# Gathered rows used a block later, two U blocks more ahead of the W build, and gated rows on ScalarE, in a decoder block with product-key experts

## The chip, the cores and the metric

The kernel runs on one core of a Trainium2 chip. The metric is the device time of one execution in microseconds (us), the median over several executions. One more execution was recorded by the hardware profiler; every row below is of that one.

## What is computed

One decoder layer over 512 tokens of width 1024, all float32: a normalisation, two token mixers side by side (differential attention and a chunked mLSTM), an output projection, and then a feed-forward part with 16,384 single-neuron experts. Each of 8 heads scores the token against two sets of 128 keys, takes the best 16 of each, combines them, keeps the best 16 of the sums, and weighs those experts by a softmax. The change concerns this last part:

```python
def peer_ffn(h, w_q, sub_keys, U, V):
    q = (h @ w_q).reshape(T, 8, 2, 128)
    # 16 best keys of each half, 16 best pairs -> eidx (expert numbers), gate (softmax of the scores)
    ...
    act = gelu(einsum('td,thkd->thk', h, U[eidx]))
    y = einsum('thk,thkd->td', act * gate, V[eidx])
```

U and V have 16,384 rows of 1024 numbers; expert number = 128 * (first key) + (second key).

## The kernel before

**Two ways to the same sum.** The first 128 tokens (block 0) have their rows of U and V fetched: there are 128 slots a token, so 128 gathers of U rows and then 128 of V rows, each an indirect DMA that brings one row of 4 KB to each of the 128 partitions (`gather`, L925, issued by GpSimd, POOL in the profile). VectorE (DVE) uses each gathered tile with one instruction of 128x1024: L931 multiplies it with the tokens' rows of h (`hrow`) and adds up to one number of `act`; L941 adds act times the row to the output `yg`. The gathered tiles lie in five rooms (`NGB`, tag "g").

The other 384 tokens are computed densely, over all experts, in 128 steps n1 of 128 experts each. `up(n1)` loads a U block of 512 KB by SP's queue (`raw_U`), ScalarE (ACT) makes its rounded high half `hi_U` (L991), DVE the rest `lo_U` (L992), TensorE (PE) makes 24 matmuls "act" (L1000 to L1002), and ACT takes their gelu into `ga` (L1004). Then the V block of the same step is loaded and split (`hi_V`, `lo_V`, L138), `ga` is multiplied by the block's gates W (L1031) and split (`ahi`, `alo`), and PE makes 18 matmuls "y" (L1046) that add to six sums in PSUM. `NGA` is 32: so many `ga` tiles exist, so that U blocks can run ahead of the V blocks.

**The gates W.** Before any y can start, the gates must be spread into W, which has a number for each token and expert. That is done in 48 blocks (`build_w`): DVE makes `onehot` (L867) and `gated` (L871), each 128x2048 in f16. One half of `gated` holds the high part of the gate in the place of the key, the other half the low part. PE makes 16 matmuls `wps` (L876, L877) of them, and ACT brings the result to a tile `st` and, for the first keys, to W0 (L883, L882). `st` goes to memory, and W comes back from there piecewise (L1025, SP's queue). While W is built, PE's free time goes to U blocks.

**The gathers' pace.** In `up`, a copy of one column of `lo_U` on POOL (`pace`, L994) stands ahead of the gathers that belong to this step (`gstep`, from n1 = 16 on 256 gathers over 111 steps, 2.3 a step); they are issued after it.

**What sets the order.** The program is written with tiles. A scheduler orders each engine's instructions once, when the program is built; on the chip each engine runs its list in that order, and waits for data and for rooms. A tag's `bufs` says how many rooms its tiles share: a tile that takes a room waits for the last reader of the tile before it.

**The rows of h.** Ahead of the scores of the keys, `hrow` is made at L892 to L896: DVE adds the halves of h (`hs4`), PE transposes four tiles, ACT copies to `hrow`, twice. `hs4` lies in one of the two rooms of tag "qt", which next hold `qt`, the transposed queries (L767), from which PE makes the key scores `pkeys` (L770), from which DVE takes the best 16 (`top16`, L753 to L757). `jcol` (L739) is a list 0 to 127 that POOL's iota makes; DVE casts it (L740, L742).

## Time and profile before

| | |
|---|---|
| Time, median of 3 runs | 1936.19 us (1936.87, 1919.65, 1936.19) |
| Profiled execution: its own time | 1931.02 us |
| Its span, first to last instruction | 1929.2 us |
| PE busy | 1814.1 us (94%) |
| DVE busy | 1428.4 us (74%) |
| ACT busy | 811.1 us (42%) |
| POOL busy | 685.8 us (36%) |
| Chain that ended last | PE 58%, DVE 18%, DMA 9%, ACT 5%, issue 5%, POOL 4% |
| Mean granted TensorE clock | 0.978 |

The busy shares are averages over stages with different limits. The feed-forward part begins near 643 us; its key scores and selections fill 650 to 800 us, the W build with the first U blocks about 800 to 957 us, and the V blocks with the remaining U blocks and all gathers the rest. A row of the chain that ended last tells who released whom, back from the last instruction.

### The profile page before, as it was taken

What the parts mean: (1) busy time and instruction counts of PE and PEld (TensorE: products, weight loads), DVE (VectorE), ACT (ScalarE), POOL (GpSimd) and SP (SyncE); (2) the same over time, 40 slices, a digit from 0 to 9 for tenths busy, and PEclk for the clock granted to TensorE, in tenths of its full rate; (3) what the DMA queues carried; (4) which work ended last, traced back from release to release, by engine and by line L of the source; (5) the groups of instructions that cost most, each with busy time, mean ns of one, the idle gap of its engine ahead of it and who ended that gap; (6) DMA issues with size and microseconds to landing.
All of it is one profiled execution on the core that took longest, in us unless ns stands there. A gap on an engine that the chain in (4) does not pass through costs nothing.

```text
span 1929.2 us, 28915 instructions
## 1 busy us (share of the span) xinstructions
PE 1814.1 (94%) x10751; PEld 1632.3 (85%) x10751; DVE 1428.4 (74%) x2732; ACT 811.1 (42%) x1359; POOL 685.8 (36%) x608
## 2 busy tenths in 40 slices
PE   5999899899998998999699999999999899999997
PEld 4989799798986888999688888899898788888886
DVE  7664746645556799999889888887776667776777
ACT  5565464463562423555434333333333233333332
...
GB/s 283 129 69 81 138 59 158 112 63 148 71 88 98 75 102 99 117 239 247 265 302 153 339 355 349 317 337 336 323 285 247 276 299 274 273 295 246 321 283 132
DMA packets 160283, 404.26 MB, mean 210 GB/s; under 512 B 14471, under 2 KB 63368, under 8 KB 160142
## 3 DMA queue, kind: packets, MB, share of 16 engines
...
HBM read 373.52 MB, written 28.84 MB: 209 GB/s over the span
## 4 chain that ended last, share of the span: by engine, by line
PE 58%; DVE 18%; DMA 9%; ACT 5%; issue 5%; POOL 4%; SPq 0%; DVEq 0%; POOLq 0%; ACTq 0%
PE y L1046 20%; PE act L1002 7%; PE act L1000 7%; PE act L1001 7%; DMA gath<-V,idx 4%; DMA ada_w<-ada_w 3%; POOL gath L925 2%; DVE lo_U L992 2%; DVE ada_acc L219 1%; DVE lo_V L138 1%; PE wps L876 1%; PE wps L877 1%; DVE ga L699 1%; ACT p L489 1%; DVE gm L701 1%
## 5 line engine op out<-in xcount | busy, mean ns | idle before, releaser
L1002 PE MATMUL act<-h_hi,lo_U 128*128 128x384 f32 x1024 | 347.1, 339 | 16.9 <-DVE lo_U L992 16.7
L1000 PE MATMUL act<-h_hi,hi_U 128*128 128x384 f32 x1024 | 345.0, 337 | 2.6 <-ACT ga L1004 2.2
L1001 PE MATMUL act<-h_lo,hi_U 128*128 128x384 f32 x1024 | 344.3, 336 | 0.0
L994 POOL COPY pace<-lo_U 128x1 f32<-128x1 f32 x128 | 99.9, 782 | 572.8 <-DVE lo_U L992 572.1
L941 DVE SCALAR_TENSOR_TENSOR yg<-gath,act,yg 128x1024 f32<-128x1024 f32 x127 | 163.0, 1283 | 111.2 <-DMA gath<-V,idx 110.6
L1046 PE MATMUL y<-lo_V,ahi 128*128 128x512 f32 x762 | 241.2, 397 | 2.6 <-DVE lo_V L138 2.6
L137 ACT CAST hi_V<-raw_V 128x1024 fp32r<-128x1024 f32 x128 | 134.3, 1050 | 245.9 <-PE y L1046 207.3
L1046 PE MATMUL y<-hi_V,alo 128*128 128x512 f32 x762 | 233.9, 395 | 1.0 <-DVE alo L138 1.0
L1046 PE MATMUL y<-hi_V,ahi 128*128 128x512 f32 x762 | 222.4, 397 | 6.0 <-ACT ahi L137 4.2
L925 POOL DMA_INDIRECT gath<-U,idx x128 | 177.1, 1383 | 130.1 <-DVE junk L931 99.3
L1002 PEld LDWEIGHTS act<-h_hi,lo_U 128*128 128x128 f32 x1024 | 192.8, 188 | 25.3 <-DVE lo_U L992 20.6
L1000 PEld LDWEIGHTS act<-h_hi,hi_U 128*128 128x128 f32 x1024 | 192.9, 188 | 8.5 <-ACT ga L1004 3.1
L1001 PEld LDWEIGHTS act<-h_lo,hi_U 128*128 128x128 f32 x1024 | 192.7, 188 | 4.3
L138 DVE TENSOR_TENSOR lo_V<-raw_V,hi_V 128x1024 fp32r<-128x1024 f32 x128 | 155.8, 1219 | 41.9 <-ACT hi_V L137 39.0
L991 ACT CAST hi_U<-raw_U 128x1024 fp32r<-128x1024 f32 x128 | 134.2, 1049 | 111.4 <-PE act L1001 98.6
L137 ACT CAST ahi<-ga 128x384 fp32r<-128x384 f32 x127 | 65.0, 512 | 271.0 <-DVE ga L1031 140.3
L1046 PEld LDWEIGHTS y<-hi_V,alo 128*128 128x128 f32 x762 | 142.5, 187 | 35.4 <-DVE alo L138 1.9
L1046 PEld LDWEIGHTS y<-lo_V,ahi 128*128 128x128 f32 x762 | 142.8, 188 | 35.0 <-DVE lo_V L138 3.6
L992 DVE TENSOR_TENSOR lo_U<-raw_U,hi_U 128x1024 fp32r<-128x1024 f32 x128 | 156.4, 1222 | 19.4 <-ACT hi_U L991 13.3
L1046 PEld LDWEIGHTS y<-hi_V,ahi 128*128 128x128 f32 x762 | 142.0, 189 | 33.3 <-ACT ahi L137 4.8
L925 POOL DMA_INDIRECT gath<-V,idx x128 | 149.4, 1167 | 35.3 <-issue 31.5
L931 DVE SCALAR_TENSOR_TENSOR junk<-gath,hrow 128x1024 bf16<-128x1024 f32 x128 | 156.0, 1219 | 4.4 <-DMA gath<-U,idx 3.5
...
## 6 DMA issues: line engine op xcount, KB each, us to landing
raw_U<-UT SPq DMA_DIRECT2D x128, 512.0 KB
raw_V<-V SPq DMA_DIRECT2D x128, 512.0 KB
...
```

The source lines that it names most:

```text
L137: A.copy(hi, src)
L138: eng.tensor_tensor(lo, src, hi.bitcast(F32), op=OP.subtract)
L925: G.indirect_dma_start(out=t_, out_offset=None, in_=src, in_offset=bass.IndirectOffsetOnAxis(ap=idx0[:, s:s + 1], axis=0))
L931: V.scalar_tensor_tensor(junk2, u, 1.0, hrow, op0=OP.mult, op1=OP.mult, accum_out=act[:, s:s + 1])
L941: V.scalar_tensor_tensor(yg, v, act[:, s:s + 1], yg, op0=OP.mult, op1=OP.add)
L991: A.copy(hi, raw)
L992: V.tensor_tensor(lo, raw, hi.bitcast(F32), op=OP.subtract)
L994: with tc.issue_after(G.tensor_copy(pace, lo[:, 0:1].bitcast(F32)).ins):
L1000: T.matmul(ps, hi[:, ks], h_hi[:, k], start=(k == 0), stop=False)
L1001: T.matmul(ps, hi[:, ks], h_lo[:, k], start=False, stop=False)
L1002: T.matmul(ps, lo[:, ks], h_hi[:, k], start=False, stop=(k == KD - 1))
L1046: T.matmul(ys[d][j], l[:, tsl], r[:, j * 512:(j + 1) * 512], start=(m == 0 and i == 0), stop=(m == KEYS - 1 and i == 2))
```

## The change

It has three parts.

**Later use.** `up` no longer uses a gathered tile where it is gathered. Tiles are put on a list `landing`, and are used in the next call of `up`, behind that block's `lo_U` in DVE's order. Tag "g" gets a sixth room (`NGB` 6).

**Two more U blocks ahead.** The gelu results of U blocks 0 and 1 no longer take two of the 32 `ga` rooms, but lie in the 4 KB room that `hrow` had (`ga01`). The rows of h go to memory instead: `hrow_out` takes a room of tag "qt", and two DMAs on ACT's queue write it to `hrow_dram` (256 KB each); one DMA on SP's queue loads it back at n1 = 2, once both `ga01` tiles have been read. `jcol` moves to tag "qt", too.

**ScalarE makes low rows.** In every fourth of the 48 W blocks (b % 4 == 2, 12 of them), DVE makes the high half of `gated` alone (128x1024), and ACT makes the low half in 8 instructions of 128x128, each a multiplication by a column of `glo`. `glo` is made by one more DVE instruction of 128x128 for each of 3 token blocks.

```diff
--- before.py
+++ after.py
@@ -41,7 +41,7 @@
     (O_QA + hp * 256,), (O_KA + hp * 256,), (O_VA + hp * 256,), (O_QM + hp * 128, O_KM + hp * 128),
     (O_VM + hp * 256,), (O_OM + hp * 256,), (O_GM + hp * 256,), (O_GA + hp * 256,))]
 NGA = 32
-NGB = 5
+NGB = 6
 QB = 1
 RB = 6
 STB = 2
@@ -719,11 +719,12 @@
     W_dram = dram.tile([NB, P, KEYS - NR, WB], F32, name="W_dram")
 
     dp = ctx.enter_context(tc.tile_pool(name="dense", bufs=1))
-    hrow = dp.tile([P, D], F32, name="hrow")
+
+    ga01 = dp.tile([P, D], F32, tag="hrow", bufs=1, name="ga01")
     idx0 = dp.tile([P, NS], I32, name="idx0")
     gate0 = dp.tile([P, NS], F32, name="gate0")
+    hrow_dram = dram.tile([P, D], F32, name="hrow_dram")
     s0_dram = dram.tile([P, NH, 2, KEYS], F32, name="s0_dram")
-    jcol = dp.tile([P, KEYS], I32, name="jcol")
 
     off_c, doff_c, iota_c = [dp.tile([P, TOPK], F16, name=n) for n in ("off_c", "doff_c", "iota_c")]
     w0pool = ctx.enter_context(tc.tile_pool(name="w0", bufs=1, side="right"))
@@ -736,6 +737,7 @@
     n21T = rp.tile([P, XT // TB, 2, TB, 2], F16, name="n21T")
     ghl = rp.tile([P, XT // TB, 2, TB, 2], F16, name="ghl")
     iota16 = rp.tile([P, KEYS], F16, name="iota16")
+    jcol = rp.tile([P, S], F32, tag="qt", bufs=2, name="jcol").bitcast(I32)[:, 0:KEYS]
     G.iota(jcol, pattern=[[1, KEYS]], base=0, channel_multiplier=0)
     V.tensor_copy(iota16, jcol)
     iota_rep = bc(iota16[:, None, :], [P, 2 * TB, KEYS])
@@ -853,12 +855,18 @@
             V.tensor_copy(n21T[:, bs, 1 - i], bc(src[:, :, :, None], [P, P // TB, TB, 2]))
         gp = bc(ps[:, 2 * P:3 * P].rearrange("p (b t) -> p b t", t=TB)[:, :, :, None], [P, P // TB, TB, 2])
         V.tensor_scalar(ghl[:, bs, 0], gp, GS, None, op0=OP.mult)
+        glo[t] = rp.tile([P, P], F32, tag="glo", bufs=2, name="glo")
+        V.scalar_tensor_tensor(glo[t].rearrange("p (b t) -> p b t", t=TB), ps[:, 2 * P:3 * P].rearrange(
+            "p (b t) -> p b t", t=TB), GS, ghl[:, bs, 0, :, 0], op0=OP.mult, op1=OP.subtract)
         V.scalar_tensor_tensor(ghl[:, bs, 1], gp, GS, ghl[:, bs, 0], op0=OP.mult, op1=OP.subtract)
 
+    glo = {}
+
     def build_w(t):
 
 
-        for b in range((t - DBS[0]) * P // TB, (t + 1 - DBS[0]) * P // TB):
+        cs0 = (t - DBS[0]) * P
+        for b in range(cs0 // TB, (cs0 + P) // TB):
             tag, dt = (("w_hi1", F32R), ("w_lo1", F32R), ("w_raw1", F32))[b % 3 if b < 2 * NB - RB else b % 2]
             pairs = [wpool.tile([P, D], dt, tag=tag, bufs=2, name=n).bitcast(F16).rearrange(
                 "p (a t n) -> p a t n", a=2, t=TB) for n in ("onehot", "gated")]
@@ -868,9 +876,13 @@
                             iota_rep.rearrange("p t (n u) -> p t n u", u=2),
                             bc(n21T[:, b].rearrange("p a t u -> p (a t) u")[:, :, None, :], [P, 2 * TB, KEYS // 2, 2]),
                             op=OP.is_equal)
-            V.tensor_tensor(pairs[1].rearrange("p a t (n u) -> p a t n u", u=2),
-                            bc(e1.rearrange("p t (n u) -> p t n u", u=2)[:, None], [P, 2, TB, KEYS // 2, 2]),
-                            bc(ghl[:, b][:, :, :, None, :], [P, 2, TB, KEYS // 2, 2]), op=OP.mult)
+            na = 1 if b % 4 == 2 else 2
+            V.tensor_tensor(pairs[1][:, 0:na].rearrange("p a t (n u) -> p a t n u", u=2),
+                            bc(e1.rearrange("p t (n u) -> p t n u", u=2)[:, None], [P, na, TB, KEYS // 2, 2]),
+                            bc(ghl[:, b, 0:na][:, :, :, None, :], [P, na, TB, KEYS // 2, 2]), op=OP.mult)
+            if na == 1:
+                for i in range(TB):
+                    A.activation(r_lo[:, i], e1[:, i], AF.Copy, scale=glo[t][:, b * TB + i - cs0:b * TB + i + 1 - cs0])
             ps = ps_sc.tile([P, TB, KEYS], F32, tag="sc", name="wps")
             for i in range(TB):
                 T.matmul(ps[:, i], e2[:, i], r_hi[:, i], start=True, stop=False)
@@ -893,7 +905,9 @@
         ps = tr_tile("hrow")
         for k in range(4):
             T.transpose(ps[:, k * P:(k + 1) * P], hs4[:, k], ident)
-        A.copy(hrow[:, k4 * 512:(k4 + 1) * 512], ps)
+        row = rp.tile([P, S], F32, tag="qt", bufs=2, name="hrow_out")
+        A.copy(row, ps)
+        A.dma_start(hrow_dram[:, k4 * 512:(k4 + 1) * 512], row)
 
     for h in range(4):
         scores(h)
@@ -926,15 +940,13 @@
                              in_offset=bass.IndirectOffsetOnAxis(ap=idx0[:, s:s + 1], axis=0))
         return t_
 
-    def gather_u(s):
-        u = gather(a["U"], s)
-        V.scalar_tensor_tensor(junk2, u, 1.0, hrow, op0=OP.mult, op1=OP.mult, accum_out=act[:, s:s + 1])
+    def use_u(s, u):
+        V.scalar_tensor_tensor(junk2, u, 1.0, hrow[0], op0=OP.mult, op1=OP.mult, accum_out=act[:, s:s + 1])
         if s == NS - 1:
             A.activation(act, act, AF.Gelu)
             V.tensor_tensor(act, act, gate0, op=OP.mult)
 
-    def gather_v(s):
-        v = gather(a["V"], s)
+    def use_v(s, v):
         if s == 0:
             V.tensor_scalar(yg, v, act[:, 0:1], None, op0=OP.mult)
         else:
@@ -977,7 +989,9 @@
         V.scalar_tensor_tensor(idx0[:, gs], idg.rearrange("p h k -> p (h k)"), float(KEYS),
                                idl.rearrange("p h k -> p (h k)"), op0=OP.mult, op1=OP.add)
 
-    gsteps = [(gather_u, s) for s in range(NS)] + [(gather_v, s) for s in range(NS)]
+    hrow = []
+    gsteps = [(f, n, s) for f, n in ((use_u, "U"), (use_v, "V")) for s in range(NS)]
+    landing = []
     h_hi, h_lo = h2_hi[:, :, d0:d0 + XT], h2_lo[:, :, d0:d0 + XT]
 
     def gstep(n1):
@@ -986,33 +1000,45 @@
     def up(n1):
 
         raw, hi, lo = wtiles(0, f"U{n1}", gpool.tile([P, D], F32, tag="rawU", bufs=NRU, name="raw_U")
-                             if n1 >= NGA + 4 else None)
+                             if n1 >= NGA + 6 else None)
         nc.sync.dma_start(raw, a["UT"][n1])
         A.copy(hi, raw)
-        V.tensor_tensor(lo, raw, hi.bitcast(F32), op=OP.subtract)
+
+        with tc.issue_after(V.tensor_tensor(lo, raw, hi.bitcast(F32), op=OP.subtract).ins):
+            while landing:
+                f, s, t_ = landing.pop(0)
+                f(s, t_)
         pace = dp.tile([P, 1], F32, tag="pace", bufs=4, name="pace")
         with tc.issue_after(G.tensor_copy(pace, lo[:, 0:1].bitcast(F32)).ins):
-            for f, s in gsteps[gstep(n1):gstep(n1 + 1)]:
-                f(s)
+            for f, n, s in gsteps[gstep(n1):gstep(n1 + 1)]:
+                landing.append((f, s, gather(a[n], s)))
+        if n1 == KEYS - 1:
+            while landing:
+                f, s, t_ = landing.pop(0)
+                f(s, t_)
         ps = acc_tile("act")[:, 0:XT]
         for k in range(KD):
             ks = slice(k * P, (k + 1) * P)
             T.matmul(ps, hi[:, ks], h_hi[:, k], start=(k == 0), stop=False)
             T.matmul(ps, hi[:, ks], h_lo[:, k], start=False, stop=False)
             T.matmul(ps, lo[:, ks], h_hi[:, k], start=False, stop=(k == KD - 1))
-        ga = dp.tile([P, XT], F32, tag="ga", bufs=NGA, name="ga")
+        ga = (ga01[:, n1 * XT:(n1 + 1) * XT] if n1 < 2 else
+              dp.tile([P, XT], F32, tag="ga", bufs=NGA, name="ga"))
         A.activation(ga, ps, AF.Gelu)
         return ga
 
     Ws = W0, W1
     gas, vparts = {}, []
     for n1 in range(KEYS):
+        if n1 == SG[0] - 1:
+            hrow.append(dp.tile([P, D], F32, tag="hrow", bufs=1, name="hrow"))
+            nc.sync.dma_start(hrow[0], hrow_dram)
         if n1 in SG:
             select_gather(4 * SG.index(n1))
         for u in range(n1, n1 + 1) if n1 < KEYS - SKEW else range(n1, KEYS) if n1 == KEYS - SKEW else ():
             gas[u] = up(u)
         ga = gas.pop(n1)
-        odd = n1 % 2 if n1 >= NGA + 4 else 0
+        odd = n1 % 2 if n1 >= NGA + 6 else 0
         vraw, vhi, vlo = wtiles(
             0 if n1 == KEYS - 1 else 1, f"V{n1}", wpool.tile([P, D], F32, tag=f"w_raw{1 - odd}", bufs=2, name="raw_V"))
         nc.sync.dma_start(vraw, a["V"][n1 * P:(n1 + 1) * P, :])
```

**What it moves, first place: DVE in the stage of the V blocks.** Each name ends in the number of its tile. Before, from one use (L941) to the next `lo_U` but one; `lo_U_15672` paces two gathers on POOL:

```order
L941 SCALAR_TENSOR_TENSOR yg<-gath,act,yg 128x1024
L992 TENSOR_TENSOR lo_U_15672<-raw_U,hi_U_15671 128x1024
L1031 TENSOR_TENSOR ga<-ga,W_9153 128x384
L941 SCALAR_TENSOR_TENSOR yg<-gath,act,yg 128x1024
L138 TENSOR_TENSOR alo<-ga,ahi 128x384
L941 SCALAR_TENSOR_TENSOR yg<-gath,act,yg 128x1024
L138 TENSOR_TENSOR lo_V_15572<-raw_V,hi_V_15571 128x1024
L941 SCALAR_TENSOR_TENSOR yg<-gath,act,yg 128x1024
L138 TENSOR_TENSOR lo_V_15643<-raw_V,hi_V_15642 128x1024
L941 SCALAR_TENSOR_TENSOR yg<-gath,act,yg 128x1024
L138 TENSOR_TENSOR lo_V_15713<-raw_V,hi_V_15712 128x1024
L941 SCALAR_TENSOR_TENSOR yg<-gath,act,yg 128x1024
```

Counted through the orders of POOL and DVE, the last two uses here are of the two gathers that `lo_U_15672` paces, with no other `lo_U` between; the two before them are of the block ahead. Of the change, one turn of three steps, on DVE (uses are L953 now):

```order
L1007 TENSOR_TENSOR lo_U_15492<-raw_U,hi_U_15491 128x1024
L953 SCALAR_TENSOR_TENSOR yg<-gath,act,yg 128x1024
L1057 TENSOR_TENSOR ga<-ga,W_6501 128x384
L953 SCALAR_TENSOR_TENSOR yg<-gath,act,yg 128x1024
L1007 TENSOR_TENSOR lo_U_15563<-raw_U,hi_U_15562 128x1024
L138 TENSOR_TENSOR alo<-ga,ahi 128x384
L1057 TENSOR_TENSOR ga<-ga,W_6501 128x384
L953 SCALAR_TENSOR_TENSOR yg<-gath,act,yg 128x1024
L138 TENSOR_TENSOR alo<-ga,ahi 128x384
L953 SCALAR_TENSOR_TENSOR yg<-gath,act,yg 128x1024
L1007 TENSOR_TENSOR lo_U_15635<-raw_U,hi_U_15634 128x1024
```

and POOL's pace and gathers of the same blocks:

```order
L1012 COPY pace<-lo_U_15421 128x1
L939 DMA gath<-V,idx_6491 128x1024 x2
L1012 COPY pace<-lo_U_15492 128x1
L939 DMA gath<-V,idx_6491 128x1024 x2
L1012 COPY pace<-lo_U_15563 128x1
L939 DMA gath<-V,idx_6491 128x1024 x3
```

The two uses behind `lo_U_15563` are of the two gathers paced by `lo_U_15492`, a block earlier. Over the 128 gathers of V, counted in the orders, the number of `lo_U` that stand between a gather's own and its use was 0 in 47 cases, 1 in 71 and 2 in 10; it is 1 in 112 cases and 2 in 16.

**Second place: ACT at the rows of h**, just behind the output projection (`wq` are the query weights). Before:

```order
L137 CAST hi_wq_4_6741<-raw_wq_4_6740 128x1024
L896 COPY hrow<-hrow 128x512
L767 COPY qt<-pr_wq_0_6583 128x512
L896 COPY hrow<-hrow 128x512
L767 COPY qt<-pr_wq_1_6658 128x512
L772 COPY s_6582<-pkeys 128x128 x2
```

Of the change:

```order
L137 CAST hi_wq_4_6746<-raw_wq_4_6745 128x1024
L909 COPY hrow_out<-hrow 128x512
L910 DMA hrow_dram<-hrow_out 128x512
L909 COPY hrow_out<-hrow 128x512
L910 DMA hrow_dram<-hrow_out 128x512
L769 COPY qt<-pr_wq_0_6588 128x512
L769 COPY qt<-pr_wq_1_6663 128x512
L774 COPY s_6587<-pkeys 128x128 x2
```

Both copies of the queries now stand behind both copies of the rows of h, and in the rooms of tag "qt" that those two stores read: the rooms hold, in turn, `jcol`, the second `hs4`, the second `hrow_out` and the second `qt` in one, and the first `hs4`, the first `hrow_out` and the first `qt` in the other.

**Third place: DVE at the end of the W build.** Before, the last three U blocks there, with 11 W blocks behind the last:

```order
L992 TENSOR_TENSOR lo_U_11671<-raw_U_11669,hi_U_11670 128x1024
L867 TENSOR_TENSOR onehot<-iota_6507,n21T 128x2048
L871 TENSOR_TENSOR gated<-onehot,ghl 128x2048
L867 TENSOR_TENSOR onehot<-iota_6507,n21T 128x2048 x2
L992 TENSOR_TENSOR lo_U_11742<-raw_U_11740,hi_U_11741 128x1024
L871 TENSOR_TENSOR gated<-onehot,ghl 128x2048
L867 TENSOR_TENSOR onehot<-iota_6507,n21T 128x2048
L871 TENSOR_TENSOR gated<-onehot,ghl 128x2048 x2
```

Of the change, to the end of the build:

```order
L1007 TENSOR_TENSOR lo_U_11991<-raw_U_11989,hi_U_11990 128x1024
L875 TENSOR_TENSOR onehot<-iota_6507,n21T 128x2048
L880 TENSOR_TENSOR gated<-onehot,ghl 128x2048
L875 TENSOR_TENSOR onehot<-iota_6507,n21T 128x2048
L880 TENSOR_TENSOR gated<-onehot,ghl 128x2048
L875 TENSOR_TENSOR onehot<-iota_6507,n21T 128x2048
L880 TENSOR_TENSOR gated<-onehot,ghl 128x1024
L875 TENSOR_TENSOR onehot<-iota_6507,n21T 128x2048
L880 TENSOR_TENSOR gated<-onehot,ghl 128x2048
L138 TENSOR_TENSOR lo_V_9300<-raw_V,hi_V_9299 128x1024
```

The row of 128x1024 is a W block of which ACT makes the other half. On PE, 36.0 instead of 34.0 U blocks stand ahead of the last W block and the first y, and 8 instead of 12 W blocks stand behind the last of these U blocks.

## Rows read from the trace of the kernel before

**Rows 1.** Windows: stretch, length, busy us (x instructions) of PE, PEld, DVE, ACT, POOL; granted clock; DMA share; GB/s.
```profile
690.00:953.00 263.00, 243.99 (x1825) 227.59 (x1823) 257.29 (x732) 123.24 (x209) 53.35 (x40) 0.97 0.52 177
850.00:900.00 50.00, 50.00 (x473) 48.02 (x471) 47.99 (x43) 28.90 (x51) 9.54 (x9) 1.00 0.74 258
925.00:957.00 32.00, 19.16 (x209) 16.94 (x206) 28.21 (x25) 16.90 (x31) 1.12 (x1) 0.72 0.69 253
1100.00:1200.00 100.00, 100.00 (x472) 86.22 (x472) 86.00 (x128) 35.58 (x48) 60.52 (x47) 1.00 0.97 359
```

**Rows 2.** Windows of the late V stage: one of five stretches, and the sum of the five.
```profile
1500.00:1600.00 100.00, 94.94 (x462) 84.45 (x461) 68.00 (x69) 31.56 (x44) 36.85 (x37) 0.98 0.83 288
...
sum 500.00, PE 483.97 PEld 433.70 DVE 351.48 ACT 166.18 POOL 182.64; mean PE 96.79 PEld 86.74 DVE 70.30 ACT 33.24 POOL 36.53
```

**Rows 3.** Waits, 1400 to 1900 us: engine line <- released by: total us, times, longest.
```profile
DVE yg L941 <- DMA gath<-V,idx: 110.6, 66, 5.1
...
PE act L1002 <- DVE lo_U L992: 12.8, 7, 4.7
```

**Rows 4.** Timeline of PE's longest wait there: start, us, engine, operation [idle before <- releaser].
```profile
1539.34 1.28 DVE L941 SCALAR_TENSOR_TENSOR yg<-gath,act,yg 128x1024 f32<-128x1024 f32 x1 [3.39 <-DMA gath<-V,idx]
...
1541.67 1.22 DVE L992 TENSOR_TENSOR lo_U<-raw_U,hi_U 128x1024 fp32r<-128x1024 f32 x1
...
1542.95 0.69 PE L1002 MATMUL act<-h_hi,lo_U 128*128 128x384 f32 x1 [4.73 <-DVE lo_U L992]
```

**Rows 5.** Chain that ended last, in order of time: start, us, what; a gather, then matmuls.
```profile
1530.74 8.50 DMA gath<-V,idx
...
1543.63 0.32 PE act L1000
...
1546.69 0.17 PE act L1001
```

**Rows 6.** Timeline of PE in the W build, across 20 act matmuls.
```profile
896.16 0.34 PE L1000 MATMUL act<-h_hi,hi_U 128*128 128x384 f32 x1
...
899.63 0.23 PE L876 MATMUL wps<-gated,onehot 128*128 128x128 f16 x1
```

**Rows 7.** Chain that ended last: a store of 256 KB, and a V block's 18 matmuls.
```profile
613.70 2.01 DMA x_dram<-x
...
1499.80 4.19 PE y L1046 x18
```

**Rows 8.** DVE by line and shape, 800 to 960 us: count, busy us, mean ns, idle before.
```profile
L871 DVE TENSOR_TENSOR gated<-onehot,ghl 128x2048 f16<-128x2048 f16 x48 | 57.1, 1216 | 0.1
...
L806 DVE TENSOR_TENSOR ge<-pos,iota_c 128x1024 f16<-128x1024 f16 x2 | 1.4, 682 | 0.0
```

**Rows 9.** ACT by line and shape, the whole span: two kinds of 128x128.
```profile
L579 ACT ACTIVATE W<-pw,RT 128x128 f32<-128x128 f32 x32 | 9.1, 369 | 7.5 <-PE pn L583 5.5 <-PE pw L575 1.9
...
L772 ACT COPY s<-pkeys 128x128 f32<-128x128 f32 x16 | 4.2, 265 | 25.9 <-PE pkeys L770 25.9
```

**Rows 10.** Timeline at the rows of h.
```profile
642.69 3.49 DVE L892 TENSOR_TENSOR hs<-h_hi,h_lo 128x512 f32<-128x512 f32 x2
...
645.59 0.23 POOL L739 IOTA jcol<- 128x128 int32 x1
...
645.87 0.58 ACT L896 COPY hrow<-hrow 128x512 f32<-128x512 f32 x1
...
646.99 1.16 PE L770 MATMUL pkeys<-keysT,qt 128*128 128x128 f32 x8
```

**Rows 11.** Timeline at the first V blocks: first y, a split's last part, the first selection.
```profile
958.86 1.22 PE L1046 MATMUL y<-hi_V,ahi 128*128 128x512 f32 x2 [3.52 <-ACT ahi L137]
...
961.46 1.02 DVE L138 TENSOR_TENSOR alo<-ga,ahi 128x384 fp32r<-128x384 f32 x2
...
971.00 1.26 DVE L753 MAX8 room<-s 128x8 f32<-128x128 f32 x6 [3.60 <-DMA s<-s_dram]
```

**Rows 12.** Windows of the uses of U rows alone: DVE busy (x instructions), ACT busy, clock, DMA share, GB/s.
```profile
1100.00:1200.00 100.00, 47.54 (x79) 0.00 (x0) 1.00 0.97 359
```

## The prediction

> **What bounds the kernel now.** I read the windows first, then the waits, then the timeline at the longest wait. In the W build (690 to 953 us) DVE is busy 257.29 of 263 us and PE 243.99 [rows 1]: DVE bounds it, except where PE is full itself (850 to 900). Its end is poor: from 925 to 957 PE is busy 19.16 of 32 us, at a granted clock of 0.72, since no U block is left to fill with. From 1100 to 1200 PE is full, with DVE at 86.00, 40 uses of U rows (79 records, two to a use) and DMA at 0.97 [rows 1, 12]; nothing is to be had there but a loss. From 1400 to 1900 PE is busy 483.97 of 500 us [rows 2], so 16.0 us are idle though DVE, at 351.48, has room. The waits say why: DVE waits 66 times and 110.6 us for gathered V rows, and PE waits 12.8 us in 7 pieces for `lo_U` [rows 3]. The timeline shows one of these: a gather issued at 1530.74 takes 8.50 us [rows 5]; its use begins at 1539.34 after 3.39 us idle, `lo_U` stands behind it in DVE's list and runs at 1541.67, and PE starts at 1542.95 after 4.73 us idle [rows 4]. After that wait, matmuls come every 0.32 us until 1546.5 and then every 0.17 [rows 5]: the lower of the clock's two levels, 1.2 GHz, after the idle time, then 2.4. That is 9 matmuls at 0.15 us extra, 1.5 us more for a long wait.
>
> **The change part by part**, against the profiled execution's own 1931.02 us; the median of the runs shown, 1936.19, lies 5 us above it, and the same differences taken from it would give times 5 us later.
>
> (a) *Later use.* 47 of the 128 V uses stood with no `lo_U` between the gather's own and the use; now all have at least one. A step of V stage lasts two blocks on PE: a U block of 24 matmuls, 3.47 us over 20 of them [rows 6], so 0.1735 each and 4.16 a block, and a V block of 4.19 [rows 7], 8.35 us together. In the new order three `lo_U` stand in a turn of three steps (25 us), 5.5 us or so apart by DVE's work between them (a `lo_U` of 1.22, two uses of 1.28 [rows 4], a smaller multiplication, and some wait). A gather of 8.50 us would still make its use wait some us, but the turn holds 25 − 17.6 us (DVE at 351.48 of 500 [rows 2]) = 7.4 us of room, and the three `lo_V` at its end now have few uses between them. So I expect DVE's waits for V rows to shrink to a third, not to nothing, and PE's for `lo_U` to all but go: 12.8 us and two or three times 1 us of slow clock, **−15**. Bounds: 0 if the waits only move, −18 if all 16.0 idle us and the slow clock go.
>
> By the Trainium skill, "DMA: Bandwidth & Descriptors", Anatomy of one DMA, a transfer issued by GpSimd takes 2.0 us and its bytes at 436 GB/s, for 512 KB an estimated 3.2 us, and no use a block behind would ever wait. The row's 8.50 us does not agree with it, and I go by the row; by the page the term would be −18.
>
> (b) *Two U blocks moved into the build.* 36 instead of 34 lie ahead of the first y. PE has 12.8 us idle from 925 to 957 [rows 1], so 48 matmuls of 0.1735 us [rows 6] fit: **−8.3** off the part behind. Bounds: −4 (only one fits), −12 (the W blocks beside them run at the full clock too: 19.16 us at 0.72).
>
> (c) *Low rows on ScalarE.* DVE's 128x2048 product takes 1.216 us; of half that size 0.682 [rows 8]. 12 × 0.534 = −6.4. Three `glo` of 128x128, below the 0.682 of a larger one each [rows 8], +1 in all; two more `lo_U` at 1.22 [rows 4], +2.4. Sum −3.0; since DVE is the bound of the build's end, it passes on: **−3**. Eight 128x128 instructions on ACT: the nearest rows are 0.369 us, a product with scale, and 0.265, a copy [rows 9]; 2.1 to 3.0 us a block, 25 to 35 us in all, where ACT is busy 28.90 of 50 [rows 1]. They hide; without that cover, were ACT the last at a block, each would cost 3.0 − 0.5 = 2.5. W block 46, the last but one, is of this kind and DVE has no U block left by then, so one such delay may show: bounds −5 and 0.
>
> A rule speaks against this part: the Trainium skill, "ScalarE: Activation LUTs", Rules for kernel authors, wants a multiplication on VectorE, not ScalarE. The row shows ACT with 21 us of 50 to spare, so the sum takes nothing for it; what ACT would cost if it bounded here is rival E.
>
> (d) *Rows of h by memory.* Both `qt` copies now wait in ACT's list behind both copies of the rows and, through the rooms, for the landing of two stores. Before, the first rows' copy ran at 645.87 and PE's scores at 646.99 [rows 10]. A store of 256 KB took 2.01 us elsewhere [rows 7]; in addition the second `hs4` waits for the iota of 645.59 and its casts, as its room is `jcol`'s [rows 10]. First copy out about 646.4, landing 648.5 to 649, the copy to `qt` as long as the other, 0.58, scores at 649.2 to 650.5. Behind them stand all the key scores, on which first PE and then DVE depend: **+3**, bounds 0 (later idle time of PE takes it up) and +5 (both stores and the iota in a row).
>
> (e) *Rows of h back.* SP's list now holds the load of `hrow` ahead of `s` and W's loads, and it waits for the splits of the first two `ga` (961.46 and 1.02 us [rows 11]). Behind it wait the selection (971.00, released by `s` [rows 11]) and W. **+1**, bounds 0 and +2.
>
> (f) *U stage.* The lead of two more blocks puts off the pacing U blocks, so that the gathers catch up at V blocks 40 to 64 instead of before 52: 48 uses in 24 V blocks and 5 U blocks, 24 × 4.19 + 5.3 × 4.16 = 122.6 us, 39 uses in 100 us. 1100 to 1200 ran 40 with PE full [rows 1, 12], so **+1**, bounds 0 and +10. The sixth room costs nothing: it takes none from another tile.
>
> Sum: −15 − 8.3 − 3 + 3 + 1 + 1 = −21.3, so 1931.0 − 21.3 = 1909.7, taken as **1909**.
>
> **The rivals.**
>
> A, *the gather waits only move.* A use a block later may wait at its new place, in front of the next `lo_U`, as spacing of 5.5 us is less than 8.50 [rows 5]. Against it: the 7.4 us of room in a turn. If it holds, (a) is near 0 and the rest gives −7: **1925**.
>
> B, *slower: the gathers of U become the bound.* In the stretch of (f) DMA would have to carry what it carried at 0.97 of its time [rows 1], for longer, with gathers in six rooms beside two more U blocks' V and W loads. DVE's room there is 122.6 × 0.14 = 17 us less what PE's order fixes, about 9. With uses 1 us late each, 48 − 9 = +39 against the gain of 21: **1949**. It decides against the change from a mean wait of (9 + 21)/48 = 0.63 us a use. Against it: PE did not wait in 1100 to 1200 at the same rate.
>
> C, *all of it.* PE's idle time from 1400 on goes with its slow clock (−18), the end of the build closes up (−12 and −4), the stores hide (+1), the rest −1: −34, **1897**. (By the page's 3.2 us for a gather, the first of these terms is due.)
>
> D, *nothing.* The scheduler's order only moves idle time about, (d) is at +5 and W's low rows are late: about **1931**.
>
> E, *ACT is last at the W blocks whose low rows it makes.* Then each of the 12 is 2.5 us later instead of 0.53 earlier: 12 × 2.5 = 30 and the 6.4 lost, so −21 + 36 = +15, **1946**. Against it: ACT's 28.90 of 50 [rows 1], and two rooms for each tile. (This is what the page's rule for ScalarE would do here.)
>
> **How the numbers follow.** Forecast (−14 to −29, so 1902 to 1917) 0.52, C 0.17, A 0.16, B 0.07, D 0.06, E 0.02. The range leaves out B, E, most of D and the far end of C: 1890 to 1929. The likeliest's own range is 1902 to 1917. One per cent, about what a measurement of this kernel can tell from no change, is 19 us: C and three quarters of the forecast are faster by more (0.17 + 0.39 = 0.56); a quarter of it, A, D and a part of B and E are within (0.13 + 0.16 + 0.06 + 0.04 = 0.39); the rest of B and E is slower, 0.05.
>
> **What would show it.** (a): DVE's wait for V rows below 50 us and PE's for `lo_U` below 4 us from 1400 to the end, PE busy 98% or more there. (b), (c): no stretch of PE idle at the build's end over 6 us, the first y about 3 us earlier than 958.86 [rows 11], counted without (d), and two more U blocks ahead of it. (d): first key scores at 649 to 651. (e): `hrow`'s load lands before the first use, the first selection at most 2 us later behind the first y. (f): DVE's wait for U rows stays below 10 us and PE full through the catch-up. Wrong it would be if PE's idle time in the V stage stayed near 16 us (A), or if a new wait of DVE for U rows stood in front of `lo_U` or `lo_V` (B).

## The result, and the profile after

The change made the kernel faster by about 1.1%: 1913.22 us (median of 11 runs, 1908.87 to 1918.74) against 1935.95 us before (11 runs, 1919.65 to 1942.41), ratio 0.9893, 95% interval 0.987 to 0.9916. Forecast were 1909 us, between 1890 and 1929, by a sum of -21 us; the medians differ by 22.7 us. The time, the range and the sign came out as forecast. Of the six terms of the sum, though, four had the wrong size, and their errors cancelled in part; the traces and the experiments show it.

The profiled execution of the changed kernel took 1913.73 us (span 1911.8), 17.3 us less than that of before.

| | before | after |
|---|---|---|
| Profiled execution | 1931.02 us | 1913.73 us |
| PE busy | 1814.1 us (94%) | 1811.8 us (95%) |
| DVE busy | 1428.4 us (74%) | 1421.3 us (74%) |
| ACT busy | 811.1 us (42%) | 838.5 us (44%) |
| PE idle from 1400 us on | 16.0 of 500 us (to 1900) | 0.1 of 480 us (to 1880) |
| DVE's waits for V rows, 1400 to 1900 us | 110.6 us | 49.0 us |
| First y | 958.86 us | 965.93 us |

The windows of the changed kernel that answer to [rows 1] and [rows 2], in the same columns; 932 to 964 is added, as the build ends 7 us later here:

```profile
690.00:953.00 263.00, 252.77 (x1871) 236.44 (x1870) 253.78 (x748) 150.38 (x300) 49.83 (x42) 0.99 0.52 176
850.00:900.00 50.00, 50.00 (x476) 47.95 (x475) 45.89 (x45) 38.90 (x89) 5.46 (x8) 1.00 0.73 258
925.00:957.00 32.00, 26.94 (x282) 25.50 (x280) 30.43 (x28) 22.57 (x50) 3.54 (x4) 0.95 0.81 300
932.00:964.00 32.00, 24.38 (x246) 21.91 (x245) 27.12 (x26) 24.20 (x54) 2.42 (x3) 0.84 0.72 275
1100.00:1200.00 100.00, 100.00 (x500) 89.91 (x499) 87.79 (x131) 36.23 (x50) 64.39 (x53) 1.00 0.98 362
...
1500.00:1600.00 100.00, 99.89 (x503) 89.91 (x502) 75.47 (x79) 36.02 (x50) 40.71 (x42) 1.00 0.88 303
...
sum 480.00, PE 479.89 PEld 433.78 DVE 349.98 ACT 167.56 POOL 192.29; mean PE 95.98 PEld 86.76 DVE 70.00 ACT 33.51 POOL 38.46
```

The end of the build is better filled, but not full. In the same 32 us (925 to 957) PE is busy 26.94 us where it had 19.16, at a granted clock of 0.95 instead of 0.72. Measured from the first y, which comes 7 us later, the like stretch is 932 to 964: 24.38 us at 0.84. From 1400 us on PE has no idle time to speak of. And 1100 to 1200 is still full, with DMA at 0.98.

Waits of the changed kernel from 1400 to 1900 us, which answer to [rows 3]:

```profile
POOL pace L1012 <- DVE lo_U L1007: 249.2, 51, 13.0
...
DVE yg L953 <- DMA gath<-V,idx: 49.0, 41, 3.1
...
PE y L1072 <- ACT hi_V L137: 1.0, 1, 1.0
```

The row of PE waiting for `lo_U`, 12.8 us before, is gone. DVE still waits 41 times for gathered rows, for 49.0 us, and PE pays nothing for it.

**Where the 17.3 us come from.** I cut both traces at the same events: the end of the last `h_lo` on DVE (the feed-forward part begins there), PE's first matmul of the second head's scores, DVE's first `onehot`, the first y and the end of the last y.

| from, to | before, us | after, us | difference |
|---|---|---|---|
| start to the last `h_lo` | 642.65 | 640.88 | -1.8 |
| last `h_lo` to second head's scores | 16.99 | 25.50 | +8.5 |
| to first `onehot` | 147.26 | 147.10 | -0.2 |
| to first y (two U blocks more in it) | 151.96 | 152.45 | +0.5 |
| to the end of the last y | 958.35 | 933.61 | -24.7 |

The first line lies ahead of everything that the change touches; over all kernels below this point lies anywhere between 638.4 and 645.8 us. The lengths behind it repeat better, and I compare kernels by the length from the last `h_lo` to the end of the last y, called **the length** below: 1274.6 us before, 1258.7 after. Each length is of one profiled execution; the changed kernel, profiled a second time (`after_again`), had 1257.0, so a difference of 2 us between two lengths says little.

The five lines make 17.7 us; the tail behind the last y took 0.3 us more.

The last line splits in the same way. Of its 24.7 us 8.3 are the two U blocks that moved ahead. The rest is time that PE lost: the sum over its matmuls of the distance from start to start, less the distance at the full clock with no wait (0.173 us for act, 0.233 for y), where that is over 0.02 us. It was 4.7 us in the first 50 us behind the first y, 1.5 from there to 1400 and 22.1 from 1400 on; it is 8.8, 1.0 and 2.1.

### The profile page after: what moved, and what is told of

Its sections match the earlier page's. It is cut to its first block, busy times and chain, and to the rows that moved or that the text cites. A ratio compares the mean times of both kernels' runs of the same rounds, so it can differ in the third digit from the quotient of the medians.

```text
span 1911.8 us, 29037 instructions
## 1 busy us (share of the span) xinstructions
PE 1811.8 (95%) x10751; PEld 1632.2 (85%) x10751; DVE 1421.3 (74%) x2735; ACT 838.5 (44%) x1455; POOL 694.5 (36%) x608
## 5 line engine op out<-in xcount | busy, mean ns | idle before, releaser
L1072 PE MATMUL y<-hi_V,ahi 128*128 128x512 f32 x762 | 218.0, 398 | 4.6 <-ACT ahi L137 3.5
L939 POOL DMA_INDIRECT gath<-U,idx x128 | 183.4, 1433 | 92.7 <-DVE junk L944 69.5
L953 DVE SCALAR_TENSOR_TENSOR yg<-gath,act,yg 128x1024 f32<-128x1024 f32 x127 | 162.7, 1281 | 49.4 <-DMA gath<-V,idx 49.0
L1007 DVE TENSOR_TENSOR lo_U<-raw_U,hi_U 128x1024 fp32r<-128x1024 f32 x128 | 156.3, 1221 | 22.7 <-ACT hi_U L1005 15.1
```

Source lines behind the costliest of these rows:

```text
L939: G.indirect_dma_start(out=t_, out_offset=None, in_=src, in_offset=bass.IndirectOffsetOnAxis(ap=idx0[:, s:s + 1], axis=0))
L953: V.scalar_tensor_tensor(yg, v, act[:, s:s + 1], yg, op0=OP.mult, op1=OP.add)
L1007: with tc.issue_after(V.tensor_tensor(lo, raw, hi.bitcast(F32), op=OP.subtract).ins):
L1072: T.matmul(ys[d][j], l[:, tsl], r[:, j * 512:(j + 1) * 512], start=(m == 0 and i == 0), stop=(m == KEYS - 1 and i == 2))
```

## The experiments

Twelve kernels ran, in three groups; the kernels of a group ran on one chip, beside runs of the kernel before. "Gap" is the time that PE lost from 1400 us on, reckoned as above. The ratio is the one on record for the runs of a group; it differs from the ratio of the two medians by up to 0.002.

| kernel | median, us | ratio to before, 95% interval | length, us | second head's scores | first y to last y | gap |
|---|---|---|---|---|---|---|
| before | | | 1274.6 | 16.99 | 958.35 | 22.1 |
| the change | 1913.22 | 0.9893 (0.987 to 0.9916) | 1258.7 | 25.50 | 933.61 | 2.1 |
| `late_only` | 1909.5 | 0.9887 (0.9863 to 0.991) | 1252.3 | 16.98 | 936.13 | 0.2 |
| `ahead_only` | 1920.33 | 0.9946 (0.9924 to 0.9967) | 1264.9 | 24.05 | 939.86 | 11.4 |
| `low_only` | 1930.43 | 0.9994 (0.9978 to 1.0011) | 1272.9 | 19.56 | 955.65 | 10.6 |
| `rows_late` | 1907.22 | 0.9879 (0.9856 to 0.9902) | 1252.8 | 15.89 | 931.49 | 0.2 |
| `late5` | 1911.69 | 0.9913 (0.9887 to 0.994) | 1253.7 | 17.00 | 937.63 | 0.8 |
| `room6` | 1920.76 | 0.9944 (0.9919 to 0.997) | 1265.7 | 17.00 | 949.63 | 11.5 |
| `rows_late_no46` | 1903.64 | 0.9868 (0.9827 to 0.9909) | 1249.1 | 16.22 | 928.30 | 0.0 |
| `rows_late_nolow` | 1905.15 | 0.988 (0.984 to 0.9919) | 1250.4 | 15.87 | 928.86 | 0.5 |
| `after_again` | 1914.39 | 0.9903 (0.9873 to 0.9934) | 1257.0 | 24.01 | 932.40 | 0.0 |
| `no46` | 1910.38 | 0.9887 (0.9855 to 0.9919) | 1253.5 | 23.97 | 930.77 | 1.1 |
| `hrow_n8` | 1903.98 | 0.9844 (0.9814 to 0.9874) | 1248.3 | 15.88 | 927.56 | 0.0 |
| `sg48` | 1904.89 | 0.9845 (0.9814 to 0.9877) | 1250.1 | 15.87 | 930.01 | 0.2 |

### The three parts alone

**Later use alone** (`late_only`): the kernel before with this part of the diff, and nothing else.

```diff
-NGB = 5
+NGB = 6
...
-        V.tensor_tensor(lo, raw, hi.bitcast(F32), op=OP.subtract)
+        with tc.issue_after(V.tensor_tensor(lo, raw, hi.bitcast(F32), op=OP.subtract).ins):
+            while landing:
+                f, s, t_ = landing.pop(0)
+                f(s, t_)
...
-            for f, s in gsteps[gstep(n1):gstep(n1 + 1)]:
-                f(s)
+            for f, n, s in gsteps[gstep(n1):gstep(n1 + 1)]:
+                landing.append((f, s, gather(a[n], s)))
```

> The kernel before with the later use and the sixth room alone; U blocks, rows of h and gated rows as before. If the later use is what emptied the V stage of PE's waits: against before -16 to -20 us (ratio 0.990 to 0.992), PE idle from 1400 us to the last y from 22 us to 2 to 4, DVE's waits for V rows from 110.6 us to about 50. If the two U blocks ahead are needed for it (a longer lead of the U blocks): -8 or less, and PE still waits for lo_U over 5 us there.

It measured 0.9887, about 22 us less, somewhat more than the first theory's 16 to 20: the whole gain of the change. Windows from 1400 to 1870 us, and waits from 1400 to 1900:

```profile
sum 470.00, PE 470.00 PEld 424.22 DVE 346.98 ACT 163.95 POOL 195.18; mean PE 94.00 PEld 84.84 DVE 69.40 ACT 32.79 POOL 39.04
```

```profile
DVE yg L939 <- DMA gath<-V,idx: 45.6, 33, 3.6
```

PE has no idle time at all, with 34 U blocks ahead as before. So the U blocks' longer lead isn't needed for it.

**Two U blocks ahead alone** (`ahead_only`): the kernel before with `ga01`, the rows of h by memory, `jcol` in the queries' room and `NGA + 6`.

```diff
-    hrow = dp.tile([P, D], F32, name="hrow")
+    ga01 = dp.tile([P, D], F32, tag="hrow", bufs=1, name="ga01")
...
-                             if n1 >= NGA + 4 else None)
+                             if n1 >= NGA + 6 else None)
```

> The kernel before with the two more U blocks ahead alone, with the rows of h by memory; uses right behind their gathers and gated rows as before. If the rows' trip costs 8 us, as the first scores in the changed kernel's trace suggest, and the two blocks give 8.3: against before 0, within -3 to +3, second head's scores at 666 us, V stage still with some 20 us of PE idle. If the trip costs the 3 us that were forecast: -4 to -6, second head's scores at 661 to 663.

It measured 0.9946, 10 us less, and neither theory had that. The rows' trip cost 24.05 - 16.99 = 7.1 us (first theory), the two blocks gave their 8.3, and there is a third effect that neither named: PE's lost time from 1400 us on fell to half, 11.4 us from 22.1, though uses stand behind their own gathers as before (in the orders, 49 of 128 with no `lo_U` between, 47 before).

```profile
DVE yg L945 <- DMA gath<-V,idx: 98.6, 60, 5.0
...
PE act L1007 <- DVE lo_U L997: 8.0, 10, 1.8
```

These waits of the same stretch say how: DVE waits nearly as long as before (98.6 us for 110.6), but PE's waits are many and short, at most 1.8 us, where before one was 4.7 [rows 3, 4].

**ScalarE's low rows alone** (`low_only`): the kernel before with `glo`, `na` and the 8 activations; as `glo` needs 1 KB, `jcol` goes to the queries' room here as well.

```diff
+            na = 1 if b % 4 == 2 else 2
...
+            if na == 1:
+                for i in range(TB):
+                    A.activation(r_lo[:, i], e1[:, i], AF.Copy, scale=glo[t][:, b * TB + i - cs0:b * TB + i + 1 - cs0])
```

> The kernel before with ScalarE's low rows alone, and the list of key numbers in the room of the queries (no memory is left for it elsewhere); rows of h as before. If DVE's saved time passes to the end of the build as forecast: -3 to -6 us, W's last block out at 951 to 954 us instead of 956.93. If it is eaten by the low rows of the last but one W block, which stand behind an evacuation on ScalarE: 0, within -2 to +2. If the list in the queries' room costs by itself: the first scores come over 1 us later than before.

It measured 0.9994, no change. From the first `onehot` to the first y it took 150.4 us where before took 152.0, so the low rows do shorten the build, by 1.6 us and not by 3 to 6. The list in the queries' room cost more than that, as the third theory had it: first scores 5.4 us behind the last `h_lo` instead of 4.3, 1.1 later, and the second head's 19.56 instead of 16.99, 2.6 later. The 1.5 us that came between are matmuls at a granted clock of 0.60 (646 to 650 us), behind idle time of PE. Here, too, the gap from 1400 us on is 10.6 instead of 22.1, and PE lost 7.2 us instead of 1.5 between the first 50 us and 1400.

The parts alone give 22 + 10 + 1 = 33 us, and the change gives 21 to 23. They overlap: `ahead_only` gains 10.7 us from 1400 us on, and `low_only` 11.5, which the later use takes anyway. On top of the later use, the other two parts in the form of the change are worth nothing that these runs show (0.9893 and 0.9903 against 0.9887).

### What the later use consists of

`late5` is `late_only` without the sixth room, `room6` is the kernel before with it and nothing else:

```diff
-NGB = 5
+NGB = 6
```

> The later use alone with five rooms for gathered rows instead of six. If it is the place of the use in DVE's order that counts: as with six rooms, ratio 0.988 to 0.990 to before. If the sixth room is needed, since seven rows are under way in a turn of three steps and a gather then waits for the room of a row that is used a block later: half the gain or less, ratio 0.994 to 0.997, with new waits of POOL's gathers for DVE's uses of V rows.

> The kernel before with a sixth room for gathered rows and nothing else. If the place of the use counts: no change, ratio 0.998 to 1.002, DVE's waits for V rows from 1400 us near 110 us. If more rows under way are enough: ratio 0.993 or less and the waits at 60 us or less.

The later use with five rooms has a length of 1253.7 us, as with six (1252.3), and the same waits; its ratio of 0.9913 overlaps with 0.9887. The feared waits of POOL's gathers for rooms of V rows don't show. So the place of the use in DVE's order is what empties the V stage.

`room6` was to change nothing, and gained 0.0056, 11 us. Its waits from 1400 us on:

```profile
DVE yg L941 <- DMA gath<-V,idx: 95.9, 54, 5.3
...
PE act L1002 <- DVE lo_U L992: 7.3, 6, 2.1
```

That is the picture of `ahead_only`: DVE waits on, PE's waits are shorter, and the gap is 11.5. Three kernels (`ahead_only`, `low_only`, `room6`) with little in common but another order of DVE's list, dealt out anew by the scheduler, halve the gap of before; and their counts of uses with no `lo_U` between are 49, 50 and 49. In two of them part of it came back ahead of 1400 us, where PE lost 7.2 us (`low_only`) and 4.1 (`room6`) instead of 1.5. What each of them changed in the list that matters was not tried, and whether the sixth room by itself helps `room6` is not shown either: POOL's gathers of V rows waited for a room for 3.8 us before and 3.6 us there. What the runs support is this: some 11 us of the 22 were waits that each of these three orders avoided, and the other 11 went with the later use alone.

### The rows of h by memory

**Rows of h behind the scores** (`rows_late`): the block that makes and stores the rows of h is moved behind the first four heads.

```diff
+    for h in range(4):
+        scores(h)
     gsl = slice(GB * P, (GB + 1) * P)
     for k4 in range(2):
...
-    for h in range(4):
-        scores(h)
```

> The changed kernel with the rows of h made and stored behind the scores of the first four heads instead of ahead of them. If the trip through memory cost 8 us because the queries' copies stood behind two stores where PE and DVE had nothing else: 6 to 8 us less than the changed kernel, ratio to before 0.985, first W block out some 7 us earlier than 824.66. If the delay is taken up later by idle time anyway, or the trip costs the same where it stands now: no change, ratio 0.989.

It measured 0.9879 and 1907.22 us. The second head's scores came 15.89 us behind the last `h_lo` instead of 25.50, so the delay at the scores is gone to the last microsecond, and the first `onehot` came 7.6 us earlier. The length fell by 5.9 us, since the build took 3.9 us more from the first `onehot` to the first y; 2.3 us of that are matmuls of U blocks, which PE had worked off during the delay and which now stand in the build. By the ratios the time is 3 to 5 us less than that of the change, between the two theories.

What the delay was made of can be read in the timeline of the changed kernel, which answers to [rows 10]:

```profile
640.91 0.69 DVE L904 TENSOR_TENSOR hs<-h_hi,h_lo 128x512 f32<-128x512 f32 x1
641.02 2.83 POOL L138 TENSOR_TENSOR lo_wq<-raw_wq,hi_wq 128x1024 fp32r<-128x1024 f32 x1 [3.43 <-ACT hi_wq L137]
...
643.82 0.23 POOL L741 IOTA jcol<- 128x128 int32 x1
...
644.08 1.12 DVE L742 CAST iota<-jcol 128x128 f16<-128x128 int32 x1 [2.47 <-POOL jcol L741]
...
645.08 2.33 POOL L138 TENSOR_TENSOR lo_wq<-raw_wq,hi_wq 128x1024 fp32r<-128x1024 f32 x1
645.24 2.72 DVE L904 TENSOR_TENSOR hs<-h_hi,h_lo 128x512 f32<-128x512 f32 x1
648.01 1.12 PE L907 MATMUL hrow<-ident,hs 128*128 128x128 f32 x4 [4.35 <-DVE hs L904]
649.21 0.58 ACT L909 COPY hrow_out<-hrow 128x512 f32<-128x512 f32 x1 [4.53 <-PE hrow L907]
...
650.22 0.58 ACT L769 COPY qt<-pr_wq 128x512 f32<-128x512 f32 x1 [0.42 <-ACT hrow_out L909]
650.86 2.07 PE L772 MATMUL pkeys<-keysT,qt 128*128 128x128 f32 x8 [1.73 <-ACT qt L769]
651.90 0.58 ACT L769 COPY qt<-pr_wq 128x512 f32<-128x512 f32 x1 [1.10 <-DMA hrow_dram<-hrow_out]
```

The second `hs` waits for the casts of `jcol`, whose room it takes; `jcol` waits on POOL behind a subtraction of 2.83 us. So the second `hs` ends 7.1 us behind the last `h_lo` instead of 3.5: 3.5 us for the list in the room. That it takes 2.72 us, beside POOL's next subtraction, is no part of the delay: the kernel before has it too (shortest, median and longest of the two, in ns):

```profile
L892 DVE TENSOR_TENSOR hs<-h_hi,h_lo x2: 692/1788/2884, 642.7 to 643.3; 128x512 f32<-128x512 f32 x2
```

Both queries' copies stand behind its rows in ACT's list. The first one starts 2.3 us behind the end of the second `hs`, where it was 0.2 before: 2.1 us for the order of ACT's copies. Only the second copy, at 651.90, waits for a store, for 1.10 us, and PE came to its scores only at 659.32. Together the first scores come 9.98 us behind the last `h_lo` instead of 4.34, 5.6 us later.

The other 2.9 of the 8.5 us are PE's clock. Behind the idle times of 4.35 and 1.73 us above, its matmuls ran at the lower level, 1.2 GHz, for some 6 us. Windows of the changed kernel, then one of before:

```profile
651.00:657.00 6.00, 6.00 (x19) 5.04 (x20) 3.67 (x24) 0.85 (x2) 0.00 (x0) 0.50 0.08 29
657.00:666.00 9.00, 9.00 (x45) 7.58 (x44) 5.10 (x26) 1.91 (x3) 0.00 (x0) 1.00 0.09 29
```

```profile
647.00:660.00 13.00, 13.00 (x67) 11.07 (x68) 8.93 (x49) 3.29 (x7) 2.23 (x1) 1.00 0.30 98
```

From the first head's scores to the second's PE makes the same 63 matmuls, in 15.5 us instead of 12.7. In the profiles with a delay of 7.0 to 7.1 us (`ahead_only`, `after_again`, `no46`) the clock rose earlier, and this part is 1.4 us. So the delay is the list in the room, the order of ACT's copies and the lower clock behind the idle time that these two made; the store is none of it.

### ScalarE's low rows in the last but one W block

In the changed kernel, ACT and DVE at the build's end (first ACT, then DVE's list):

```profile
953.49 0.22 ACT L894 ACTIVATE W<-wps 128x64 f32<-128x64 f32 x1 [1.34 <-PE wps L889]
956.23 0.97 ACT L895 ACTIVATE st<-wps 128x960 f32<-128x960 f32 x1 [2.52 <-DMA W_dram<-st]
957.10 2.44 ACT L885 ACTIVATE gated<-onehot,glo 128x128 f16<-128x128 f16 x8
959.44 0.21 ACT L894 ACTIVATE W<-wps 128x64 f32<-128x64 f32 x1
```

```profile
955.89 0.69 DVE L880 TENSOR_TENSOR gated<-onehot,ghl 128x1024 f16<-128x1024 f16 x1
...
962.50 2.36 DVE L138 TENSOR_TENSOR lo_V<-raw_V,hi_V 128x1024 fp32r<-128x1024 f32 x2 [3.31 <-PE wps L889]
```

DVE has its half ready at 956.6, ACT the other at 959.5: its 8 activations stand behind an evacuation (ACT's copy of a W block's result) to `st`, which has two rooms and waits 2.52 us for a store. Two kernels leave the low rows of this block to DVE (`no46` from the change, `rows_late_no46` from `rows_late`), and one leaves all of them (`rows_late_nolow`):

```diff
-            na = 1 if b % 4 == 2 else 2
+            na = 1 if b % 4 == 2 and b < 2 * NB - 4 else 2
```

> The changed kernel without ScalarE's low rows in the last but one W block, rows of h as in the change. If these low rows are late behind the evacuation that waits for a store: first y 2 to 4 us earlier after the first W block than in the changed kernel, and 2 to 4 us less in all. If the stores set the end by themselves: no change.

> The changed kernel with the rows of h behind the first four heads' scores, and without ScalarE's low rows in the last but one W block (11 blocks of 48 instead of 12). There these low rows stand in ScalarE's list behind an evacuation that waits for a room of st, whose store is under way, so that the last two W blocks are late. If that wait holds the first y: 2 to 4 us less than with them, ratio 0.986. If the stores themselves set the end of the build: no change, ratio 0.988.

> The changed kernel with the rows of h behind the first four heads' scores, and without ScalarE's low rows in any W block: DVE makes both halves everywhere. If the low rows are worth nothing, as alone on the kernel before: ratio 0.987 to 0.989, as with them. If with two more U blocks in the build DVE bounds its end and the low rows do pay: 3 us more or above, ratio 0.990.

`no46` ran beside the change itself: 1910.38 against 1914.39 us, 4.0 us less by medians, with intervals that overlap (0.9855 to 0.9919 and 0.9873 to 0.9934). From the first `onehot` to the first y it took 151.45 us, the change 152.45 and 153.26: 1 to 1.8 us less, not 2 to 4. The rest lies behind the first y, where PE lost 5.6 us in 50 instead of 7.8 (`after_again`, the same chip). `rows_late_no46` and `rows_late_nolow` took 155.49 and 156.11 us for that, `rows_late` 156.32. So leaving this one block to DVE is worth 1 to 2 us at the first y, and the other 11 blocks of low rows less than can be measured: the kernels with and without them (`rows_late_no46` and `rows_late_nolow`) differ by 1.5 us in the median and overlap.

### Behind the first y

PE lost 8.8 us in the first 50 us behind the first y of the change, 4.7 before. Two kernels on `rows_late_no46` (6.3 us there) tried what could be late: `hrow_n8` loads the rows of h at n1 = 8 instead of 2, behind the first selection's load in SP's list, and `sg48` makes the selections at n1 = 4 and 8.

```diff
-        if n1 == SG[0] - 1:
+        if n1 == 8:
```

```diff
-SG = (3, 5)
+SG = (4, 8)
```

> Rows of h behind the first four heads' scores, no low rows in the last but one W block, and the rows of h loaded back at n1 = 8 instead of 2, which puts the load behind the first selection's in SP's list. If the load ahead of the selection is what made PE's idle time in the first 50 us behind the first y grow from 4.7 us (before) to 8.8 (the change): back to 3 to 5 us, and 2 to 4 us less in all, ratio 0.985. If the growth comes from the two U blocks that DVE and PE no longer have there to fill with: still over 6 us, no change.

> Rows of h behind the first four heads' scores, no low rows in the last but one W block, and the two selections for the gathers at n1 = 4 and 8 instead of 3 and 5, the rows of h loaded at 3. If DVE, full with both selections in one stretch, is what PE waits for behind the first y: idle time there down to 3 us, 3 to 5 us less in all, ratio 0.984. If only the order of SP's loads counts: as with the load at n1 = 8.

> The changed kernel again, beside the three below on one chip. Ratio to before 0.989 as measured, within 0.987 to 0.992.

PE lost 5.5 and 7.8 us there, the first between its two theories, the second far from the 3 us of its first, and the times, 1903.98 and 1904.89 us, are that of `rows_late_no46` (1903.64 on another chip). `after_again`, the change beside them, measured 0.9903, as expected. So neither the load's place nor both selections in one stretch makes the 6.3 us of that kernel; on the change itself neither was tried. What PE waits for there in the change is one gelu and one `lo_V`:

```profile
996.62 0.44 PE L1022 MATMUL act<-h_hi,hi_U 128*128 128x384 f32 x1 [1.18 <-ACT ga L1027]
...
999.13 1.22 PE L1072 MATMUL y<-lo_V,ahi 128*128 128x512 f32 x2 [1.89 <-DVE lo_V L138]
```

The last row's two matmuls take 1.22 us, where such a pair takes 0.63 at the full clock (at 979.22, for one): the clock had fallen again after the two waits. From 982 to 1017 us the granted clock is 0.90 on the mean; in the 35 us of before that answer to it, 975 to 1010, it is 1.00. Before had two waits there as well, 1.00 us for the gelu and 1.28 for `lo_V`. Why `lo_V` is later stays open. The profiles on record point at two of the change's parts, without a test of their own: with 34 U blocks ahead and no low rows in block 46, the last but one, PE lost 3.4 to 4.7 us there (four kernels), with 36 blocks 5.5 to 6.4 (five; `sg48`, with 7.8, stands outside), and with low rows in block 46 7.6 to 9.4 (`low_only`, `after_again`, the change, `rows_late`).

`hrow_n8` is the fastest of all with a comparison on one chip: 1903.98 us (1902.19 to 1907.95) against 1914.39 us of the change (1913.66 to 1916.31) and 1931.3 us of before; its ratio of 0.9844 has an interval of 0.9814 to 0.9874 (the two medians give 0.986). `sg48` and `rows_late_no46` can't be told from it. All three are the change with the rows of h behind the scores and no low rows in the last but one W block.

## Why the prediction was right, and where its steps were not

**(a) Later use: right in kind, too small.** The forecast was -15, its bounds 0 and -18. PE's lost time from 1400 us on went from 22.1 to 2.1, -20, and `late_only` shows that this needs nothing else. DVE's waits fell to 49.0 us, not to a third of 110.6 but nearly to half, and cost PE nothing, as the argument with the room in a turn said. The term that was mis-sized, beyond its own bound, is what the waits cost PE. The sum took the 12.8 us of waits for `lo_U`; idle time of every kind was 16.0 us up to 1900 [rows 2] and 0.5 behind. The other 5.6 of the 22.1 us are not mainly the lower clock, for which 2 to 3 us stood. Two of the windows behind PE's waits in the kernel before, and the timeline at the second:

```profile
1540.00:1548.00 8.00, 5.05 (x19) 5.01 (x20) 6.17 (x8) 2.36 (x4) 3.76 (x5) 0.79 0.59 200
...
1735.00:1740.00 5.00, 4.09 (x23) 4.10 (x24) 3.95 (x6) 1.17 (x3) 3.82 (x2) 1.00 0.75 224
```

```profile
1733.41 0.34 PE L1001 MATMUL act<-h_lo,hi_U 128*128 128x384 f32 x1
1735.91 0.45 PE L1002 MATMUL act<-h_hi,lo_U 128*128 128x384 f32 x1 [2.16 <-DVE lo_U L992]
1736.19 0.34 PE L1000 MATMUL act<-h_hi,hi_U 128*128 128x384 f32 x1
```

The clock fell behind the wait of 4.73 us alone and cost some 1.7 us there, as the step had it; behind every other wait of over 0.5 us it stayed at 1.00. But each wait cost about 0.27 us beyond its idle time: 0.17, since idle time is counted from the end of the matmul before, 0.34 us behind its start, where the next would start 0.17 behind it, and 0.11 more until the second matmul follows. Over a dozen waits this makes most of the rest. That half of the gain goes with any of three new orders, as `room6`, `ahead_only` and `low_only` show, stood in no step.

**(b) Two U blocks ahead: right.** 8.3 us of PE's work went from behind the first y to ahead of it (first y to last y: 36 instead of 34 blocks ahead), and the build took 0.5 us more with them in it. `ahead_only`, without low rows, took 1.7 us more. PE still idles at the build's end, less than before.

**(c) Low rows on ScalarE: wrong.** -3 was forecast, with bounds of -5 and 0. From the first `onehot` to the first y the change took +0.5 us. Beside `ahead_only` (153.69 us), which has the two U blocks and no low rows, that is 1.2 us less, and 0.4 in `after_again`: so the low rows gave 0.4 to 1.2 us, hardly more than two profiles of one kernel differ by, where -6.4 and +1 for `glo` stood in the sum. The step "since DVE is the bound of the build's end, it passes on" failed: at the last blocks of the changed kernel ACT is as late as DVE, with the low rows of block 46 behind an evacuation. PE's waits for W's products from 900 to 970 us show both, where before DVE's alone cost 11.1 us in 9 waits:

```profile
PE wps L888 <- ACT st L895: 3.1, 3, 1.8
PE wps L888 <- DVE gated L880: 2.9, 2, 1.6
```

The prediction named that very block as one where a delay might show, and left it to the bounds. What it overlooked is why: `st` has two rooms, and ACT waits for a store ahead of the low rows. ACT's mean load, 28.90 of 50 us [rows 1], says nothing of that. Alone, this part was worth 1.6 us in the build and nothing in all.

Eight products of 128x128 took ACT 2.44 us, where DVE saves 0.54 us (1220 ns for 128x2048, 684 for 128x1024 in its groups). The rule of the Trainium skill that was weighed there, "ScalarE: Activation LUTs", Rules for kernel authors, wants such products on VectorE, and these rows agree with it. Rival E's price, 2.5 us at each of 12 blocks, still did not come: without the eleven blocks ahead of block 46 the time was the same (`rows_late_no46` and `rows_late_nolow`).

**(d) Rows of h by memory: mis-sized.** +3 was forecast with a bound of +5; it was +8.5 up to the second head's scores, and 7.0 to 7.1 in three other profiles. The failing step is "First copy out about 646.4, landing 648.5 to 649": it took the store as the long piece and the iota as an addition. In truth the wait for the iota and its casts cost 3.5 us, ACT's order 2.1, and the store nothing that PE waited for. The rest, 2.9 us here and 1.4 in the three others, is PE's lower clock behind its idle time, which stood in (a) of the sum and not in (d). The sign that was asked for, first key scores at 649 to 651, came out (650.86) by luck: the part began 1.8 us earlier in this execution, and from the last `h_lo` the scores are 5.6 us later. About half of the delay was made up later by PE's U blocks, as `rows_late` shows, which the lower bound had as a mechanism.

**(e), (f): too small.** +2 was forecast. The selection began 13.8 us behind the first y instead of 12.1, 1.6 later, within (e)'s bound; but PE lost 4.1 us more in the first 50 us, and the load's place isn't the reason, as far as `hrow_n8` shows it. Part of these 4.1 us may belong to (b) and (c), as the profiles behind the first y suggest. The catch-up of the gathers of U rows (f) cost nothing: PE was full from 1100 to 1400, and DVE waited 9.8 us in all for U rows. Rival B needed 0.63 us a use; 9.8 us over 128 uses are 0.08.

**The sum.** From the last `h_lo` on: -20.0 (a), -8.3 (b), +0.5 (c), +8.4 (d), +3.6 (e, f), together -15.8, where -21.3 was forecast. The profiled execution of the change also started the feed-forward part 1.8 us earlier. That the medians differ by 22.7 us, and not by 17.3, is the 5 us by which the profiled execution of before lies below its median; the prediction had said so of its basis, and with the median of before as basis its sum gives 1914.7. So the time of 1909 us against 1913 owes part of its accuracy to luck: (a) gave 5 us more than forecast, (d) cost 5.4 and (e, f) 1.6 more, and (c) was 3.5 worse.

**What the other rivals would have shown.** A (waits only move) asked for idle time near 16 us from 1400 on: it is 0.1. C asked for the closing of the build's end, which did not come: PE still waited there, for ACT and for DVE. D fell with the result itself.
